# Hybrid decoder layer on one core: the mixing part with its norms, splits, meta columns and order of work rewritten

## The chip, the core and the metric

The kernel runs on one core of a Trainium2 chip. The metric is the device time of one execution in microseconds, given as the median of several runs; the times are from the device. TensorE (PE) multiplies matrices, VectorE (DVE) and ScalarE (ACT) work element by element, GpSimd (POOL) can do element work too and issues some transfers, SyncE (SP) issues most transfers. Each engine executes its own instructions in order and waits for the others by semaphores.

## The reference

One decoder layer over 512 tokens of width 1024, with 16 learned meta tokens in front (528 rows). What is computed:

```python
h = layer_norm(concat([meta, x]), ln_in_g, ln_in_b)
q, k, v, gb, gc, z = split(h @ w_in)            # 512 columns each
attn = differential_attention(q, k, v)          # 4 heads, two softmax maps each, causal, T5 bias
conv = gb * short_conv(gc * z, conv_w)          # depthwise, width 3, causal
mix = concat([attn, conv]) @ w_out
h = layer_norm(ALPHA * h + mix, ln1_g, ln1_b)
ffn = peer(h, w_q, sub_keys, u, v)              # per token and head: top-16 of 128 x 2 sub-keys, then experts
out = layer_norm(ALPHA * h + ffn, ln2_g, ln2_b)[16:]
```

A head's attention is softmax(map 0) - lam * softmax(map 1), times v, then an RMS norm over 128 columns. The expert stage (`peer`) needs the queries of all tokens and two top-16 selections per token and head before it can gather or weigh experts.

## The kernel before

All products are done in float16 with a high and a low half per operand: `split` writes the high half by ScalarE (`hi = scale * src`) and the low half by VectorE (`lo = scale * src - hi`); `mm3` then multiplies three times (high-high, high-low, low-high) into one PSUM bank. `split_pool` is a second form, with two ScalarE passes and the low half on GpSimd; `load_w(..., pool=True)` uses it for the four chunks (0.5 MB each) of a weight of 512 columns. Weights are split into three rotating pairs of buffers, so a weight's split can begin once the third one before it has been used up.

The order of the work: the Python program below gives each engine its instructions with a priority by program order, and a planner, which works with estimated durations, fixes the order on every engine before the run. An engine never departs from that order on the chip.

- Entry: `tile_v` for the four row tiles of 128 tokens and the 16 meta rows (i = -1): `layer_norm`, `split_rows`, transposes into `tTh`/`tTl` (`rows_to_T`), product with the value weight. Then the key and the query projections.
- Loop: 16 `units` (4 row blocks i x 4 heads h). Per unit `att_a` (scores of both maps, bias, maximum, exponentials, split into `ph` and `pl`), run two units ahead; `att_t` (transposes of the probabilities); one `fill` (a quarter of `conv_gc`, `conv_z` or `conv_gb`, or an output projection); `att_b` (times values, norm); `att_c` one unit later (transposes into `mixh`/`mixl`). The meta columns have operands of their own: 16-column transposes into `pTm`, 16-row products with `vmh`/`vml`.
- After the loop: output projections of row blocks 2 and 3 with a norm each (`out_proj`), transposes (`out_T`), the load of the first query weight of the expert stage and its product, first for 384 tokens, then for the last 128.
- Expert stage: three more query weights, sub-key scores, 64 runs of `top16` on VectorE, then the products with all experts' `u`, and at the end with all `v`. The first row tile's experts are gathered row by row through GpSimd's queue; its last norm is `layer_norm(x1[0], ...)`.

In `layer_norm` the statistics give mean and variance, `rstd` takes the power on GpSimd and one refinement step on VectorE; the normalization is one pass (VectorE, or ScalarE where `act_norm`), then times g on VectorE, then plus b (GpSimd where `pool_add`).

Of the kernel before, what the change touches and what calls it, by code (L numbers as in the profile page):

```python
# [23 lines left out]
H = 4  # L24
# [28 lines left out]
def build(tc, A, out):  # L53
# [35 lines left out]
    def layer_norm(x, n, g, b, pool_add, act_norm=False, halves=None):  # L89
        stt = small.tile([P, 2, 6], F32, name="bst")  # L90
        mv = small.tile([P, 2], F32, name="bmv")
        for c in range(2):
            V.bn_stats(stt[:n, c, :], x[:n, c * 512:(c + 1) * 512])
        V.bn_aggr(mv[:n], stt[:n])
        r = rstd(mv[:n, 1:2], n, EPS)
        if halves:
            for c in range(2):
                cs = slice(c * 512, c * 512 + 512)
                y = x[:n, cs]
                V.tensor_scalar(y, y, mv[:n, 0:1], r[:n], op0=OP.subtract, op1=OP.mult)  # L100
                V.tensor_tensor(y, y, g[:n, cs], op=OP.mult)
                V.tensor_tensor(y, y, b[:n, cs], op=OP.add)
                halves(cs)
            return
# [21 lines left out]
    def split_rows(x, n, pool, lo_eng):  # L126
# [3 lines left out]
        lo_eng.tensor_tensor(xl[:n], x[:n], xh[:n], op=OP.subtract)  # L130
# [9 lines left out]
    def load_w(src, nb, pool=False):  # L140
        wh = wst.tile([P, KT, 512], F16, name="wh")
        wl = wst.tile([P, KT, 512], F16, name="wl")
        for j in range(4):
# [3 lines left out]
            (split_pool if pool else split)(wh[:, s, :], wl[:, s, :], w, WS)  # L147
# [18 lines left out]
    with ExitStack() as s1:  # L166
# [21 lines left out]
        vmh = q.tile([NM, T], F16, name="vmh")  # L188
        vml = q.tile([NM, T], F16, name="vml")
# [13 lines left out]
        def tile_v(i):  # L203
# [3 lines left out]
            if i == 0:  # L207
# [7 lines left out]
                layer_norm(x, n, *lnv, pool_add=False, halves=half)  # L215
                rows_to_T((xh, xl), n, r0)
            else:
                layer_norm(x, n, *lnv, pool_add=i > 1, act_norm=i > 0)
                rows_to_T(split_rows(x, n, wk, G if i > 1 else V), n, r0)
# [5 lines left out]
            wv = W["v"]  # L225
            p = bank()
            mm3(p[:n], lambda k: tTh[:, k, r0:r0 + n], lambda k: tTl[:, k, r0:r0 + n],
                lambda k: wv[0][:, k, :], lambda k: wv[1][:, k, :], KT)
            if i < 0:
                split(vmh, vml, p[:n], 1.0 / WS)  # L230
            else:
                split(vh[:, i, :], vl[:, i, :], p[:n], 1.0 / WS)
# [48 lines left out]
        def conv_gc(c):  # L281
            if c == 0:
                W["gc"] = load_w(A["w_in"], 4, pool=True)
# [3 lines left out]
        def conv_z(c):  # L287
            if c == 0:
                W["z"] = load_w(A["w_in"], 5, pool=True)
# [4 lines left out]
        def conv_gb(c):  # L294
            if c == 0:
                W["gb"] = load_w(A["w_in"], 3, pool=True)
# [8 lines left out]
        def out_proj(i, nb):  # L305
            for b in range(2):
                if ("wo", b) not in W:
                    W["wo", b] = load_w(A["w_out"], b, pool=True)
# [20 lines left out]
        def att_a(i, h):  # L329
# [4 lines left out]
            for m in range(2):  # L334
                r = slice(m * DK, (m + 1) * DK)
                for f0 in range(0, w, 512):
                    f1 = min(w, f0 + 512)
                    p = bankA()
# [549 lines left out]
```

## Time and profile before

| | us |
|---|---|
| median of 3 runs | 1536.63 (1535.18 to 1537.24) |
| the profiled execution | 1538.28 |
| its span, first to last instruction | 1536.5 |
| busy in the span: PE / DVE / ACT / POOL | 1427.5 / 1220.7 / 749.5 / 376.5 |

Times in rows are microseconds from the start of the span, if no unit stands there. A busy TensorE is not TensorE at its peak: its instructions overlap, so a product's own duration is longer than its distance to the next one. Idle time before an instruction stands in brackets with what ended it.

### The profile page before, as it was taken

What the parts mean: (1) busy time and instruction counts of PE and PEld (TensorE: products, weight loads), DVE (VectorE), ACT (ScalarE), POOL (GpSimd) and SP (SyncE); (2) the same over time, 40 slices, a digit from 0 to 9 for tenths busy, and PEclk for the clock granted to TensorE, in tenths of its full rate; (3) what the DMA queues carried; (4) which work ended last, traced back from release to release, by engine and by line L of the source; (5) the groups of instructions that cost most, each with busy time, mean ns of one, the idle gap of its engine ahead of it and who ended that gap; (6) DMA issues with size and microseconds to landing.
All of it is one profiled execution on the core that took longest, in us unless ns stands there. A gap on an engine that the chain in (4) does not pass through costs nothing.

```text
span 1536.5 us, 23225 instructions
## 1 busy us (share of the span) xinstructions
PE 1427.5 (93%) x8768; PEld 764.4 (50%) x8768; DVE 1220.7 (79%) x2509; ACT 749.5 (49%) x1227; POOL 376.5 (25%) x262
## 2 busy tenths in 40 slices
PE   5799999969989979897999999999999999999994
PEld 2244545554555647574454545545455555555551
DVE  8414678649899999894788898888978888988886
ACT  5427546363245838474444444444544444444441
POOL 2334432342001223101022122222312122212213
PEclk9799999989999989999999999999999999999997
DMA  6352111070035757759899889899989999999851
GB/s 229 111 159 69 57 55 56 1 236 15 1 114 168 249 179 251 240 173 336 334 364 384 322 352 359 352 357 349 371 338 351 357 353 342 373 353 357 321 213 55
DMA packets 85989, 370.92 MB, mean 241 GB/s; under 512 B 10495, under 2 KB 15647, under 8 KB 69492
## 3 DMA queue, kind: packets, MB, share of 16 engines
q1 hardware_dynamic: 57724, 200.53, 35.9%
q0 software_dynamic: 28144, 168.90, 30.0%
q8 instruction: 68, 1.11, 0.3%
q14 instruction: 45, 0.37, 0.1%
q10 hardware_dynamic: 8, 0.01, 0.0%
HBM read 335.05 MB, written 35.69 MB: 241 GB/s over the span
## 4 chain that ended last, share of the span: by engine, by line
PE 33%; issue 21%; DVE 9%; POOL 4%; DMA 3%; POOLq 0%; ACT 0%; DVEq 0%
PE po L816 19%; PE pa L154 13%; POOL grow L671 3%; DMA grow<-peer_uv,idx 3%; DVE ul L116 2%; DVE rh L651 1%; DVE rl L652 1%; DVE oh L650 1%; DVE oh L649 1%; POOL gscr L638 1%; PE b L628 0%; DVE tci L163 0%; DVE c L161 0%; DVE tci L160 0%; DVE soh L583 0%
## 5 line engine op out<-in xcount | busy, mean ns | idle before, releaser
L154 PE MATMUL pa<-tTh,uh 128*128 128x384 f16 x1024 | 338.0, 330 | 8.9 <-ACT act L484 8.5
L154 PE MATMUL pa<-tTh,ul 128*128 128x384 f16 x1024 | 337.7, 330 | 8.8 <-DVE ul L116 8.8
L154 PE MATMUL pa<-tTl,uh 128*128 128x384 f16 x1024 | 337.6, 330 | 0.0
L671 POOL DMA_INDIRECT grow<-peer_uv,idx x128 | 175.6, 1372 | 611.0 <-DVE acc L688 546.0
L154 PEld LDWEIGHTS <-uh 128*128 128x128 f16 x2048 | 201.2, 99 | 148.8 <-issue 16.2
L116 DVE SCALAR_TENSOR_TENSOR ul<-uf,uh 128x1024 f16<-128x1024 f32 x128 | 161.8, 1264 | 100.6 <-ACT uh L115 100.5
L816 PEld LDWEIGHTS <-wwh 128*128 128x128 f16 x1488 | 145.8, 98 | 182.2 <-ACT wwh L808 12.6
L115 ACT ACTIVATE uh<-uf 128x1024 f16<-128x1024 f32 x128 | 135.2, 1056 | 202.3 <-PE pa L154 185.7
L816 PE MATMUL po<-pvh,wwh 128*128 128x512 f16 x744 | 182.1, 381 | 11.8 <-ACT pvh L115 11.1
L816 PE MATMUL po<-pvl,wwh 128*128 128x512 f16 x744 | 181.6, 380 | 0.0
L816 PE MATMUL po<-pvh,wwl 128*128 128x512 f16 x744 | 180.8, 379 | 0.0
L116 DVE SCALAR_TENSOR_TENSOR pvl<-vf,pvh 128x1024 f16<-128x1024 f32 x128 | 155.6, 1220 | 26.1 <-ACT pvh L115 26.1
L115 ACT ACTIVATE pvh<-vf 128x1024 f16<-128x1024 f32 x128 | 134.3, 1050 | 70.5 <-PE po L816 69.8
L688 DVE SCALAR_TENSOR_TENSOR acc<-grow,gact,acc 128x1024 f32<-128x1024 f32 x127 | 162.6, 1280 | 0.6 <-ACT gact L680 0.6
L678 DVE SCALAR_TENSOR_TENSOR grow<-grow,x 128x1024 f32<-128x1024 f32 x128 | 156.2, 1220 | 7.7 <-DMA grow<-peer_uv,idx 7.7
L154 PEld LDWEIGHTS <-ul 128*128 128x128 f16 x1024 | 101.2, 99 | 78.8 <-DVE ul L116 11.1
L808 ACT ACTIVATE wwh<-w 128x384 f16<-128x384 f32 x128 | 66.7, 522 | 142.4 <-DVE w L806 142.4
L154 PE MATMUL b<-tTh,wh 128*128 128x512 f16 (+4 forms) x416 | 122.8, 321 | 13.0 <-DVE tTh L138 10.5
L154 PE MATMUL b<-tTl,wh 128*128 128x512 f16 (+4 forms) x416 | 124.2, 320 | 0.0
L154 PE MATMUL b<-tTh,wl 128*128 128x512 f16 (+4 forms) x416 | 123.7, 319 | 0.0
L816 PEld LDWEIGHTS <-wwl 128*128 128x128 f16 x744 | 72.8, 98 | 87.8
L154 PEld LDWEIGHTS <-wh 128*128 128x128 f16 x832 | 69.9, 100 | 75.4 <-issue 17.4
(228 smaller groups left out, 2039.7 us busy)
## 6 DMA issues: line engine op xcount, KB each, us to landing
uf<-uT SPq DMA_DIRECT2D x128, 512.0 KB
vf<-vL SPq DMA_DIRECT2D x128, 512.0 KB
gscr<-stg POOLq DMA_DIRECT2D x12, 2048.0 KB, 13.3
gr<-gscr SPq DMA_DIRECT2D x32, 768.0 KB
w<-w_in SPq DMA_DIRECT2D x24, 512.0 KB
w<-w_q SPq DMA_DIRECT2D x16, 512.0 KB
ascr<-act POOLq DMA_DIRECT2D x18, 384.0 KB, 4.8
aload<-ascr SPq DMA_DIRECT2D x18, 384.0 KB
```

What stands on the lines that cost most here:

```text
L115: S.activation(hi, src, AF.Copy, scale=scale)
L116: V.scalar_tensor_tensor(lo, src, scale, hi, op0=OP.mult, op1=OP.subtract)
L154: m = PE.matmul(o, a(k), b(k), start=first and n == 0, stop=last and n == 3 * nk - 1)
L638: G.dma_start(gscr[:, :, (i - 1) * (P // CT) + c, :], stg.rearrange("p (g j) t -> p g (j t)", j=GG))
L649: V.tensor_tensor(pairs(o2), row, mid(gT[:, 1, ts]), op=OP.is_equal)
L650: V.tensor_tensor(pairs(o1), row, mid(gT[:, 0, ts]), op=OP.is_equal)
L651: V.tensor_tensor(pairs(rh), pairs(o2), mid(gT[:, 2, ts]), op=OP.mult)
L671: G.indirect_dma_start(out=uv, out_offset=None, in_=A["peer_uv"], in_offset=bass.IndirectOffsetOnAxis(ap=idx[:, j:j + 1], axis=0))
L678: V.scalar_tensor_tensor(uv[:, :D], uv[:, :D], 1.0, x1[0], op0=OP.mult, op1=OP.mult, accum_out=c)
L688: V.scalar_tensor_tensor(acc, uv[:, D:], c, acc, op0=OP.mult, op1=OP.add)
L808: S.activation(wh, w, AF.Copy)
L816: PE.matmul(po[i][c], x[:, ts], y[:, c * 512:(c + 1) * 512], start=f and k == 0, stop=False)
```

## The change

`layer_norm` becomes two VectorE passes, (x - mean) * g and then * rstd + b, on VectorE everywhere. `split_pool` goes: all weights are split by `split`, and the low halves of the rows and of the probabilities are taken on VectorE. GpSimd keeps the power in `rstd` and its transfers.

The 16 meta columns of a unit become one tile of 128 columns: both maps, each with (high, low) twice; one transpose gives `pTm`, and one product per map with `vm`, a zero-padded tile of 128 rows that holds the meta values' high and low halves at the matching rows (the meta rows' value product is made for 8 copies of the 16 rows, `xrep`). Scores are issued with the two maps in turn, with a bank from the second pool for columns from 512 on. `fill` is written out anew: two quarters of `conv_gc`/`conv_z` in each of the first four units, `conv_gb` in the next four, then the output projections of blocks 0, 1 and 2; the last half of the query product is put around the last output projection, and the load of the first query weight is written into unit 10.

```diff
-    def layer_norm(x, n, g, b, pool_add, act_norm=False, halves=None):
+    def layer_norm(x, n, g, b, halves=None):
...
+        for c in range(2) if halves else (None,):
+            cs = slice(0, D) if c is None else slice(c * 512, c * 512 + 512)
+            y = x[:n, cs]
+            V.scalar_tensor_tensor(y, y, mv[:n, 0:1], g[:n, cs], op0=OP.subtract, op1=OP.mult)
+            V.scalar_tensor_tensor(y, y, r[:n], b[:n, cs], op0=OP.mult, op1=OP.add)
+            if halves:
                 halves(cs)
-        if act_norm:
-            mr = small.tile([P, 1], F32, name="mr")
-            V.scalar_tensor_tensor(mr[:n], mv[:n, 0:1], -1.0, r[:n], op0=OP.mult, op1=OP.mult)
-            S.activation(x[:n], x[:n], AF.Identity, bias=mr[:n], scale=r[:n])
-        else:
-            V.tensor_scalar(x[:n], x[:n], mv[:n, 0:1], r[:n], op0=OP.subtract, op1=OP.mult)
-        V.tensor_tensor(x[:n], x[:n], g[:n], op=OP.mult)
-        (G if pool_add else V).tensor_tensor(x[:n], x[:n], b[:n], op=OP.add)
...
-    def split_pool(hi, lo, src, scale):
-        S.activation(src, src, AF.Copy, scale=scale)
-        S.activation(hi, src, AF.Copy)
-        G.tensor_tensor(lo, src, hi, op=OP.subtract)
...
-            (split_pool if pool else split)(wh[:, s, :], wl[:, s, :], w, WS)
+            split(wh[:, s, :], wl[:, s, :], w, WS)
...
+        vm = q.tile([P, H, 2, P], F16, name="vm")
+        V.memset(vm, 0.0)
...
+            if i < 0:
+                a, b = (wk.tile([P, KT, P], F16, name=f"xrep{e}", tag=t) for e, t in enumerate(("xh", "xl")))
+                for d, s in ((a, tTh), (b, tTl)):
+                    S.copy(d.rearrange("p k (r t) -> p k r t", t=NM),
+                           s[:, :, :NM].unsqueeze(2).to_broadcast([P, KT, P // NM, NM]))
...
+                for m in range(2):
+                    o = lambda r: vm[r, :, m, :]
+                    f = lambda r: p[r].rearrange("p (h d) -> p h d", h=H)
+                    r = slice(m * 64, m * 64 + 64)
+                    S.activation(o(r), f(r), AF.Copy, scale=1.0 / WS)
+                    r = slice(m * 64 + 32, m * 64 + 64)
+                    V.scalar_tensor_tensor(o(r), f(r), 1.0 / WS, o(r), op0=OP.mult, op1=OP.subtract)
...
-                last = i >= 2
-                layer_norm(x1[i], P, *lnv, pool_add=not last, act_norm=not last)
-                W["x", i] = split_rows(x1[i], P, wk, V if last else G)
+                layer_norm(x1[i], P, *lnv)
+                W["x", i] = split_rows(x1[i], P, wk)
...
+            for f0 in range(0, w, 512):
+                f1 = min(w, f0 + 512)
+                ps = [bankA() if f0 == 0 else bank() for _ in range(2)]
+                for e, (a, b) in enumerate(((qh, kh), (qh, kl), (ql, kh))):
+                    for r, p in zip(rs_, ps):
+                        PE.matmul(p[:, :f1 - f0], a[r, h, qs], b[r, h, f0:f1], start=e == 0, stop=e == 2)
...
-            S.activation(ph[:, :, :w], lg[:, :, :w], AF.Copy)
-            G.tensor_tensor(pl[:, :, :w], lg[:, :, :w], ph[:, :, :w], op=OP.subtract)
+            lm = lg[:, :, :NM].unsqueeze(2).to_broadcast([P, 2, 2, NM])
+            S.activation(pm[:, :, :, 0, :], lm, AF.Copy)
+            V.tensor_tensor(pm[:, :, :, 1, :], lm, pm[:, :, :, 0, :], op=OP.subtract)
+            S.activation(ph[:, :, :w - NM], lg[:, :, NM:w], AF.Copy)
+            V.tensor_tensor(pl[:, :, :w - NM], lg[:, :, NM:w], ph[:, :, :w - NM], op=OP.subtract)
...
-                    PE.transpose(tm[:NM, a, m, :], s[:, m, :NM], ident)
...
-            S.copy(pTm, tm[:NM, :2])
+            tm = bank(F16)
+            PE.transpose(tm[:, :P], pm.rearrange("p m r a t -> p (m r a t)"), ident)
+            S.copy(pTm, tm[:, :P])
...
-                mm3(o, lambda k: pTm[:, 0, m, :], lambda k: pTm[:, 1, m, :],
-                    lambda k: vmh[:, hs], lambda k: vml[:, hs], 1, last=False)
+                PE.matmul(o, pTm, vm[:, h, m, :], start=True, stop=False)
...
+        conv = [(f, c) for f in (conv_gc, conv_z, conv_gb) for c in range(4)]
+        fill = [conv[2 * n:2 * n + 2] for n in range(4)] + [[c] for c in conv[8:]]
+        fill += [[(out_proj, 0, 0)], [(out_proj, 0, 1)], [(out_proj, 1, 0)],
+                 [(out_proj, 1, 1), (out_T, 0)], [(out_T, 1)], [(out_proj, 2, 0)], [(out_proj, 2, 1)], []]
...
+            if n == 10:
+                wqs[0] = load_w(A["w_q"], 0)
...
-        for i in range(2, NT):
-            for nb in range(2):
-                if (i, nb) == (NT - 1, 0):
-                    att_c(*units[-1])
-                out_proj(i, nb)
-            out_T(i - 1)
-        wqs = {0: load_w(A["w_q"], 0)}
...
-        pq_mm(wqs[0], pq0, 0, 384)
+        out_T(2)
+        pq_mm(wqs[0], pq0, 0, 384, (0, 1))
+        att_c(*units[-1])
+        out_proj(3, 0)
+        out_proj(3, 1)
+        pq_mm(wqs[0], pq0, 0, 384, (2, 3))
         out_T(NT - 1)
         pq_mm(wqs[0], pq0, 384, 512)
```

## Rows read from the trace of the kernel before

**Rows 1.** Stretches: length; PE, PEld, DVE, ACT, POOL busy; clock, DMA share, GB/s.

```profile
0.00:117.00 117.00, 87.85 (x492) 39.34 (x492) 54.72 (x97) 50.70 (x64) 39.17 (x25) 0.90 0.51 164
117.00:307.70 190.70, 182.81 (x1418) 95.62 (x1418) 126.38 (x352) 106.69 (x203) 72.52 (x53) 0.96 0.15 48
307.70:346.30 38.60, 26.54 (x241) 19.29 (x240) 18.46 (x21) 23.34 (x27) 16.71 (x10) 0.87 0.71 235
346.30:440.90 94.60, 91.35 (x573) 48.40 (x573) 89.27 (x532) 29.70 (x59) 10.09 (x6) 1.00 0.06 18
440.90:700.00 259.10, 236.36 (x1876) 154.55 (x1875) 248.73 (x611) 164.28 (x203) 48.51 (x31) 0.95 0.65 209
```

**Rows 2.** Timeline of TensorE, one unit of two blocks: start, us, line, operation, count.

```profile
177.43 0.22 PE L154 MATMUL b<-vmh,pTm 16*128 16x128 f16 x1
...
178.76 0.28 PE L402 MATMUL bh<-ident,ohl 128*128 128x128 f16 x2
...
179.58 0.22 PE L364 MATMUL bh<-ident,ph 128*16 128x128 f16 x1
...
180.97 0.17 PE L154 MATMUL b<-tTh,wh 128*128 128x2 f16 x1
```

**Rows 3.** Timeline of TensorE: score products of both maps, blocks 2 and 3.

```profile
178.96 0.35 PE L154 MATMUL pa<-kh,qh 64*128 64x400 f16 x2
...
255.40 0.39 PE L154 MATMUL pa<-kh,qh 64*128 64x512 f16 x1
...
257.54 0.39 PE L154 MATMUL pa<-kh,qh 64*128 64x512 f16 x1
```

**Rows 4.** VectorE, single lines in the loop: duration ns min/median/max, first and last start.

```profile
L116 DVE SCALAR_TENSOR_TENSOR wl<-w,wh x4: 1201/1222/2425, 243.9 to 254.8; 128x1024 f16<-128x1024 f32 x4
...
L84 DVE SCALAR_TENSOR_TENSOR rt<-ry,ve x19: 210/220/2077, 135.9 to 299.5; 128x1 f32<-128x1 f32 x19
...
L299 DVE SCALAR_TENSOR_TENSOR y<-gc,cw,y x4: 748/750/2357, 169.5 to 240.2; 128x512 f32<-128x512 f32 x4
```

**Rows 5.** Timelines of GpSimd and of VectorE around 164.

```profile
163.87 2.13 POOL L121 TENSOR_TENSOR wl<-w,wh 128x1024 f16<-128x1024 f32 x1
...
163.93 2.08 DVE L84 SCALAR_TENSOR_TENSOR rt<-ry,ve 128x1 f32<-128x1 f32 x1 [0.81 <-POOL ry L83]
```

**Rows 6.** VectorE's groups in the loop: busy us, mean ns, idle before, releaser.

```profile
L84 DVE SCALAR_TENSOR_TENSOR rt<-ry,ve 128x1 f32<-128x1 f32 x19 | 7.9, 414 | 8.7 <-POOL ry L83 8.6
...
L395 DVE TENSOR_TENSOR ohl<-o,ohl 128x128 f16<-128x128 f32 x16 | 6.1, 380 | 4.1 <-ACT ohl L394 3.7
...
L383 DVE RECIPROCAL rz<-z 128x2 f32<-128x2 f32 x16 | 2.6, 163 | 4.3 <-ACT lg L347 4.2
```

**Rows 7.** Timelines of TensorE and VectorE in the hand-over.

```profile
310.24 0.81 PE L154 MATMUL b<-tTh,wh 128*128 128x384 f16 x4 [1.50 <-ACT tTh L138]
...
325.84 0.61 PE L137 MATMUL bh<-ident,xh 128*128 128x128 f16 x8
...
335.51 1.23 DVE L116 SCALAR_TENSOR_TENSOR ul<-uf,uh 128x1024 f16<-128x1024 f32 x1 [4.40 <-ACT uh L115]
336.65 0.68 DVE L138 COPY tTh<-bh 128x1024 f16<-128x1024 f16 x1
...
337.39 1.01 PE L154 MATMUL b<-tTh,wh 128*128 128x128 f16 x5 [10.50 <-DVE tTh L138]
...
346.32 0.49 DVE L159 MAX8 svt<-sc 128x8 f32<-128x128 f32 x2 [1.33 <-ACT sc L531]
```

**Rows 8.** Timeline of VectorE: eviction and split of row tile 2.

```profile
296.52 0.69 DVE L315 SCALAR_TENSOR_TENSOR x<-b,x 128x512 f32<-128x512 f32 x1 [2.27 <-PE b L154]
...
304.72 1.21 DVE L130 TENSOR_TENSOR xl<-x,xh 128x1024 f16<-128x1024 f32 x1
```

**Rows 9.** Timelines of GpSimd and ScalarE in the entry.

```profile
44.52 8.24 POOL L130 TENSOR_TENSOR xl<-x,xh 128x1024 f16<-128x1024 f32 x1 [1.17 <-ACT xh L129]
...
72.01 0.59 ACT L115 ACTIVATE vmh<-b 16x512 f16<-16x512 f32 x1 [4.25 <-PE b L154]
```

More of the change, by code (lines that the diff above doesn't have):

```diff
@@ L213, in half @@
                     V.tensor_tensor(xl[:, cs], x[:, cs], xh[:, cs], op=OP.subtract)
-                layer_norm(x, n, *lnv, pool_add=False, halves=half)
+                layer_norm(x, n, *lnv, halves=half)
                 rows_to_T((xh, xl), n, r0)
             else:
-                layer_norm(x, n, *lnv, pool_add=i > 1, act_norm=i > 0)
-                rows_to_T(split_rows(x, n, wk, G if i > 1 else V), n, r0)
+                layer_norm(x, n, *lnv)
+                rows_to_T(split_rows(x, n, wk), n, r0)
             if "v" not in W:
@@ L333, in att_a @@
             qs = slice(i * P, (i + 1) * P)
[L334 to L338, printed above, removed]
-                    mm3(p[:, :f1 - f0], lambda k: qh[r, h, qs], lambda k: ql[r, h, qs],
-                        lambda k: kh[r, h, f0:f1], lambda k: kl[r, h, f0:f1], 1)
+            rs_ = [slice(m * DK, (m + 1) * DK) for m in range(2)]
+            for f0 in range(0, w, 512):
[4 more added lines that the diff above has]
+                        PE.matmul(p[:, :f1 - f0], a[r, h, qs], b[r, h, f0:f1], start=e == 0, stop=e == 2)
+                for m, p in enumerate(ps):
                     V.scalar_tensor_tensor(lg[:, m, f0:f1], p[:, :f1 - f0], DK ** -0.5,
@@ L348, in att_a @@
                              accum_out=z[:, m:m + 1])
[L349 to L353 removed]
+            ph = wk.tile([P, 2, T], F16, name="ph", bufs=3)
+            pl = wk.tile([P, 2, T], F16, name="pl")
+            pm = wk.tile([P, 2, 2, 2, NM], F16, name="pm", bufs=3)
+            lm = lg[:, :, :NM].unsqueeze(2).to_broadcast([P, 2, 2, NM])
[3 more added lines that the diff above has]
+            V.tensor_tensor(pl[:, :, :w - NM], lg[:, :, NM:w], ph[:, :, :w - NM], op=OP.subtract)
+            pp_[i, h] = ph, pl, pm, z
         def att_t(i, h):
             nb = i + 1
[L357 removed]
+            ph, pl, pm, z = pp_.pop((i, h))
             pT = wk.tile([P, 2, 2, NT, P], F16, name="pT")
[L359 to L360 removed]
+            pTm = wk.tile([P, P], F16, name="pTm")
             for a, s in enumerate((ph, pl)):
@@ L406, in build @@
         units = [(i, h) for i in range(NT) for h in range(H)]
-        fill = [(f, (c,)) for f in (conv_gc, conv_z, conv_gb) for c in range(4)]
-        fill += [(out_proj, (0, 0)), (out_proj, (0, 1)),
-                 (out_proj, (1, 0)), (lambda: (out_proj(1, 1), out_T(0)), ())]
+        conv = [(f, c) for f in (conv_gc, conv_z, conv_gb) for c in range(4)]
+        fill = [conv[2 * n:2 * n + 2] for n in range(4)] + [[c] for c in conv[8:]]
+        fill += [[(out_proj, 0, 0)], [(out_proj, 0, 1)], [(out_proj, 1, 0)],
+                 [(out_proj, 1, 1), (out_T, 0)], [(out_T, 1)], [(out_proj, 2, 0)], [(out_proj, 2, 1)], []]
+        wqs = {}
         att_a(*units[0])
@@ L415, in build @@
             att_t(*u)
-            if fill:
-                f, args = fill.pop(0)
+            for f, *args in fill[n]:
                 f(*args)
+            if n == 10:
+                wqs[0] = load_w(A["w_q"], 0)
             att_b(*u)
@@ L421, in build, with pq_mm @@
                 att_c(*units[n - 1])
-        for i in range(2, NT):
-            for nb in range(2):
-                if (i, nb) == (NT - 1, 0):
-                    att_c(*units[-1])
-                out_proj(i, nb)
-            out_T(i - 1)
-        wqs = {0: load_w(A["w_q"], 0)}
-        pq0 = [bank() for _ in range(4)]
-        def pq_mm(w, pq, r0, r1):
-            for c in range(4):
+        pq0 = [None] * 4
+        def pq_mm(w, pq, r0, r1, cc=range(4)):
+            for c in cc:
+                if pq[c] is None:
+                    pq[c] = bank()
                 cs = slice(c * P, (c + 1) * P)
@@ L514, in build @@
             else:
-                pq = [bank() for _ in range(4)]
+                pq = [None] * 4
                 pq_mm(w, pq, 0, 512)
```

42 lines of the change are left out of this document (13 added, 29 removed).

## The prediction

> **What bounds the kernel now.** I read the table by stretches first. [rows 1] splits the span where the work changes: the entry up to the last key and query projection (0 to 117), the loop over the 16 attention units with convolution and output projection (to 307.7, the end of the last output projection), the hand-over to the retrieval queries (to 346.3, when the first top-16 starts), the top-16 stage (to 440.9), and the stretch behind it up to 700, where the work changes again and which the diff hardly touches. The reader is to see that TensorE is busy 182.8 of 190.7 us in the loop, VectorE only 126.4 and GpSimd 72.5; that in the hand-over nobody is full; and that in the top-16 stage TensorE (91.4 of 94.6) and VectorE (89.3) are both nearly full. Behind it VectorE is busy 248.7 of 259.1 us, and nothing there can begin before the top-16 values exist: so I take it that whatever is gained or lost up to 440.9 moves the end by as much.
>
> Three kinds of loss show in the first 346 us, and the instruction timelines show them. First, TensorE pays for small tiles. In one unit with two key blocks the product with the values runs from 177.43 to 178.76, 1.33 us for 18 products, and the transposes from 179.58 to 180.97, 1.39 us for 12, though two 128-column products there take 0.28 where one takes 0.22, so a pitch of 0.056 [rows 2]. The difference lies around the 16-row and 16-column operands. Second, GpSimd holds up VectorE: a one-element instruction at 163.93 lasts 2.08 us while GpSimd's subtraction (163.87, 2.13 us) runs, against a median of 0.22 [rows 4, 5]; and GpSimd's own subtraction at 44.52 takes 8.24 us [rows 9]. Third, an order: at 326 the last rows are transposed, but their copy (336.65) stands on VectorE behind a weight split (335.51) that itself waited 4.40 us, and TensorE idles 10.50 us before 337.39 [rows 7].
>
> **Entry (0 to 117).** The two-pass norm replaces, for tiles 2, 3 and the meta rows, passes spread over ScalarE, VectorE and GpSimd; row splits go to VectorE. The 8.24 us subtraction becomes one VectorE instruction of about 1.21 us (same size as the median split in [rows 4]), 7 us earlier for tile 3's transposes. Against it: two ScalarE copies that repeat the meta columns, about 1 us each, behind which the meta product waits, partly under tile 3's product; the meta product itself keeps its 24 products of 512 columns. The zeroing of the new value tile lies in the start, when VectorE waits for the input. Another 1 us comes from the shorter chain of tile 1. The last meta product, evicted at 72.01 [rows 9], comes about 8 us earlier, and the projections behind it are pure TensorE work. Bounds: 0, and -15, half of the 29 us that TensorE is idle there [rows 1]. I take -8, nearest to the 7 of the row.
>
> **Loop (117 to 307.7).** TensorE: the meta columns as one tile turn 18 products into 14 and 12 transposes into 9 for two blocks: 14 x 0.056 = 0.78 for 1.33, 9 x 0.056 = 0.50 for 1.39, so 1.44 us per unit and 23 us for 16. (The counts removed, 4 and 3, and the operand switches are the same for any number of blocks.) The alternating score maps give less than they seem to: already now the two maps start as a pair (0.35 us for two at 178.96), except in the last four units, where the first map's 512 columns begin at 255.40 and the second's at 257.54 [rows 3]. There three products of 0.22 become free: 0.65 us x 4 = 2.6. TensorE's floor is 190.7 - 26 = 165 us.
>
> VectorE gets what GpSimd loses. Splits of three weights (the third convolution weight and two output weights, four chunks each) 12 x 1.21 = 14.5; the first query weight's four are on VectorE already [rows 4]. The low half of the probabilities, 256 to 1024 elements by block: between 0.22 (one element) and 1.21 (1024) that is 0.46, 0.71, 0.96, 1.21, times four units each: 13.4. The small meta subtraction, 16 x 0.22 = 3.5. Norms behind the output projection: tiles 0 and 1 get two passes of 1.22 for one pass and a small instruction, and a split of 1.21, +4.6 together; tile 2 goes from 3.26 to 2.44, -0.8. Sum +35.2. Off goes the hold-up: in two groups alone, the 19 instructions of line 84 (mean 414 against a median of 220 ns, 3.7 us) and the four of line 299 (one of 2357 against 750, 1.6), it is 5.3 us [rows 4, 6]; I take -12 for all groups, a bit over twice that, as GpSimd keeps only one one-column power per norm of its 72.5. VectorE then has 126.4 + 35.2 - 12 = 150.
>
> [...]
>
> 150 on VectorE and 165 on TensorE would still fit side by side, but they don't lie evenly. The convolutions now come two at a time in the first four units: about 53 us of TensorE, with some 34 of VectorE. That leaves TensorE 112 and VectorE 116 for the other twelve units and the last projections. VectorE's queue is in order, and three waits stay in it: for GpSimd's power 8.6 us, for ScalarE's half 3.7 and its exponentials 4.2 [rows 6], 16.5, three quarters of it in these units: 116 + 12 = 128. So 53 + 128 = 181, a gain of 10; what is late next is VectorE. Bounds: -26 (TensorE's floor) and +5 (only 5 of hold-up back, no wait hidden). I take -10.
>
> **Hand-over (307.7 to 346.3).** Now half of the first query product, 48 products, stands ahead of the last unit's projection and half behind. From 310.24 to 325.84 is 15.6 for 96, so 7.8 each. Behind the last projection: the chain from eviction to the split runs 296.52 to 305.93 for tile 2, 9.4 us [rows 8], less 0.8 for the two-pass norm and less 0.7 for a foreign instruction inside: 7.9, under the 7.8 of product. Then transposes 0.9, two copies 1.3, and from the product's start to the first top-16 8.9 (337.39 to 346.32) [rows 7]: with the half's small surplus 19.5. If the other half and the second transposition (8.7 + 1.5 wait) aren't covered by VectorE's lag in the loop, 29.7. The stall need not go: the query weights' splits are on VectorE too now, also ahead of that copy. Bounds: -19 (19.5) and 0 (38.6, the stall as it was); I take 29.7, so -9.
>
> **Top-16 (346.3 to 440.9).** The last query weight's splits (four GpSimd instructions lie here now) cost VectorE 4 x 1.21 = 4.8, less about 1 of hold-up; 5.3 us of VectorE idle time take some. Bounds 0 and +14.5, if all twelve splits fall in here. I take +3.
>
> **After that.** The first tile's last norm loses a GpSimd pass and gains about 0.4 us of VectorE, ahead of the final rows: 0, bounds -2 and +2. Other stretches 0.
>
> Sum: -8 - 10 - 9 + 3 = -24. The profiled execution took 1538.28 us for its span of 1536.5; after, 1514.3 for 1512.5. The median of the runs is 1.65 below the profiled one: 1536.63 - 24 = **1512.6 us**.
>
> **Rivals.** (a) VectorE keeps up, its work falling into TensorE's shade: loop -26, hand-over -12, entry -8, top-16 +1, together -45: 1491.6. For it: 64 us of VectorE idle in the loop; against it: the 128 above. (b) Gains eaten: VectorE becomes the bound (loop -2), the copy again waits behind splits (hand-over 0), entry -8, top-16 +5: -5, 1531.6. For it: one queue has all the small steps. (c) Slower: the queue of VectorE in the hand-over. If the eight splits of two query weights stand ahead of the last transposes' copies and wait for their transfers (the window already moves 235 GB/s, so 2.2 us a chunk of 0.5 MB, 18 us in place of the 10.5 stall), +8 there, the third's and late ones +14.5 in the top-16 stage, loop 0, entry -8: +14.5, 1551.1. It decides once more than four splits precede the copy. Against it: splits come early when their buffers are free.
>
> [...]
>
> **How the numbers follow.** Likeliest 55%, (a) 14%, (b) 19%, (c) 9%, (d) 3%. Its own range is 1500 to 1526. The 80% range is 1494 to 1535: it leaves out half of (a), and (c) and (d). A measurement can tell about 0.2% (3 us) from no change. Faster: 55 + 14 + 12 of (b) = 81%; same: 6%, of (b); slower: 13%, (c), (d) and 1 of (b).
>
> **What would show it.** Right: a meta product evicted near 64; no 16-row products; VectorE near 150 us in the loop and fuller than TensorE in units 4 to 15, with TensorE waiting on its results; the first top-16 near 319; top-16 stage 97 us; no VectorE instruction stretched to 2 us. Wrong: TensorE still full through all units (a), the last copies behind splits (b, c), a clock well under 0.96 in the loop (d), or a different length of the stretches behind, which I hold fixed.

## The result and the profile after

The changed kernel takes 1525.36 us in the median of 4 runs (1525.21 to 1525.47), the kernel before 1536.93 beside it: a ratio of 0.9921 with a 95% interval of 0.9905 to 0.9937, a gain of 11.6 us. The profiled execution took 1525.31 us for a span of 1523.5, 13.0 less than the span before. Forecast was 24.

The table by stretches of the changed kernel, cut at the same events as [rows 1] (first score product, eviction of the last output projection, first top-16, end of the top-16 stage); its columns are those of [rows 1]:

```profile
0.00:106.60 106.60, 85.45 (x493) 38.59 (x494) 62.62 (x105) 44.98 (x59) 11.94 (x14) 0.95 0.54 185
106.60:303.20 196.60, 174.64 (x1375) 98.27 (x1375) 141.36 (x402) 86.57 (x201) 13.33 (x19) 0.92 0.15 47
303.20:328.80 25.60, 18.32 (x182) 13.54 (x181) 17.10 (x24) 12.79 (x17) 1.52 (x1) 0.87 0.77 261
328.80:427.70 98.90, 92.20 (x565) 49.04 (x563) 93.30 (x537) 29.29 (x58) 1.49 (x2) 0.98 0.10 35
```

The entry is 10.4 us shorter, the loop 5.9 longer, the hand-over 13.0 shorter, the top-16 stage 4.3 longer: together -13.2 at 427.7, and the rest of the span keeps it (1095.6 us behind that point before, 1095.8 after). The loop now holds some work that stood in the hand-over before, the third block's transposes and half of the first query product, 8.7 us by [rows 7]. Like for like the loop gained 2.8 and the hand-over 4.3.

Timelines of the changed kernel, TensorE (PE), VectorE (DVE) and ScalarE (ACT), from the meta value product over the start of the loop and one unit of two blocks to the hand-over:

```profile
62.41 0.59 ACT L227 ACTIVATE vm<-b 64x512 f16<-64x512 f32 x1 [6.89 <-PE b L139]
...
107.57 1.23 DVE L106 SCALAR_TENSOR_TENSOR wl<-w,wh 128x1024 f16<-128x1024 f32 x1 [4.73 <-ACT wh L105]
...
109.32 3.49 DVE L106 SCALAR_TENSOR_TENSOR wl<-w,wh 128x1024 f16<-128x1024 f32 x3
112.72 0.52 DVE L340 SCALAR_TENSOR_TENSOR lg<-pa,bias 128x144 f32<-128x144 f32 x2
...
113.07 0.28 PE L338 MATMUL pa<-kh,qh 64*128 64x144 f16 x1 [6.11 <-DVE lg L340]
...
185.67 0.40 PE L367 MATMUL bh<-ident,ph 128*128 128x128 f16 x4
...
186.39 0.38 PE L139 MATMUL b<-tTh,wh 128*128 128x512 f16 x1
...
191.57 0.22 PE L381 MATMUL b<-vm,pTm 128*128 128x128 f16 x1
...
192.30 0.22 PE L139 MATMUL b<-vh,pT 128*128 128x128 f16 x1
...
303.21 0.69 DVE L314 SCALAR_TENSOR_TENSOR x<-b,x 128x512 f32<-128x512 f32 x1
...
304.76 1.22 DVE L106 SCALAR_TENSOR_TENSOR wl<-w,wh 128x1024 f16<-128x1024 f32 x1
...
307.02 1.23 DVE L106 SCALAR_TENSOR_TENSOR wl<-w,wh 128x1024 f16<-128x1024 f32 x1 [0.91 <-ACT wh L105]
...
308.22 1.28 DVE L99 SCALAR_TENSOR_TENSOR x<-x,bmv,lnv 128x1024 f32<-128x1024 f32 x1
...
310.08 1.22 DVE L106 SCALAR_TENSOR_TENSOR wl<-w,wh 128x1024 f16<-128x1024 f32 x1
...
311.28 1.21 DVE L106 SCALAR_TENSOR_TENSOR wl<-w,wh 128x1024 f16<-128x1024 f32 x1
...
312.60 1.28 DVE L100 SCALAR_TENSOR_TENSOR x<-x,ry,lnv 128x1024 f32<-128x1024 f32 x1
315.00 1.23 DVE L115 TENSOR_TENSOR xl<-x,xh 128x1024 f16<-128x1024 f32 x1 [1.12 <-ACT xh L114]
```

The reader is to see three things. The small tiles came out nearly as priced: for two blocks the products with the values begin at 191.57 and the last of the 14 at 192.30 (0.78 us with its pitch, 1.33 in [rows 2]), and from the first transposes to the next product are 0.72 us (1.39 in [rows 2], 0.50 forecast), so 1.22 us a unit for a forecast of 1.44. At the start of the loop four weight splits stand on VectorE between 107.57 and 112.72, ahead of the first scores, and TensorE waits 6.11 us. And in the hand-over four splits (line 106) stand inside the norm of the last row block; from its eviction at 303.21 to the end of its split at 316.23 are 13.0 us.

The clock behind the wait at 113.07, in a table of three short stretches, and then the loop up to the fourth unit's result (170.1) and from there to the first query product (columns as above, the granted clock is the third number from the end):

```profile
106.60:113.10 6.50, 0.39 (x8) 0.25 (x9) 5.53 (x7) 4.26 (x5) 0.00 (x0) 0.87 0.42 123
113.10:117.00 3.90, 3.05 (x42) 1.95 (x42) 3.60 (x14) 3.20 (x15) 0.00 (x0) 0.50 0.89 321
117.00:121.00 4.00, 4.00 (x11) 1.38 (x10) 1.56 (x8) 1.57 (x7) 0.00 (x0) 0.50 0.03 11
...
106.60:170.10 63.50, 56.23 (x481) 29.47 (x482) 32.44 (x98) 24.06 (x67) 1.65 (x3) 0.92 0.20 67
170.10:283.40 113.30, 98.61 (x795) 58.61 (x792) 102.84 (x298) 58.35 (x130) 11.68 (x16) 0.92 0.12 38
```

Behind 6.1 us of standing still TensorE is granted half its clock (0.50 in both stretches from 113.10 to 121.00) for the next eight microseconds.

The single lines that answer to [rows 4], in the loop of the changed kernel (minimum, median and maximum in ns):

```profile
L84 DVE SCALAR_TENSOR_TENSOR rt<-ry,ve x19: 214/219/222, 133.1 to 281.5; 128x1 f32<-128x1 f32 x19
...
L106 DVE SCALAR_TENSOR_TENSOR wl<-w,wh x20: 1204/1221/1226, 107.6 to 302.1; 128x1024 f16<-128x1024 f32 x20
```

No VectorE instruction of the loop is stretched to 2 us any more; the longest takes 1.28 us.

### The profile page after: what moved, and what is told of

Its sections match the earlier page's. It is cut to its first block, busy times and chain, and to the rows that moved or that the text cites. A ratio compares the mean times of both kernels' runs of the same rounds, so it can differ in the third digit from the quotient of the medians.

```text
span 1523.5 us, 22944 instructions
## 1 busy us (share of the span) xinstructions
PE 1405.7 (92%) x8656; PEld 759.8 (50%) x8656; DVE 1247.0 (82%) x2573; ACT 712.6 (47%) x1209; POOL 281.1 (18%) x205
## 4 chain that ended last, share of the span: by engine, by line
PE 47%; DVE 21%; issue 19%; DMA 7%; POOL 4%; ACT 1%; POOLq 0%; SPq 0%; DVEq 0%; ACTq 0%
PE po L821 21%; PE pa L139 13%; PE b L139 12%; DMA grow<-peer_uv,idx 4%; DVE ul L106 2%; POOL grow L676 2%; DVE wl L106 2%; DMA gscr<-stg 1%; DVE rh L656 1%; POOL ry L83 1%; DVE rl L657 1%; DVE oh L654 1%; DMA kf<-keysT 1%; DVE oh L655 1%; POOL gscr L643 1%
## 5 line engine op out<-in xcount | busy, mean ns | idle before, releaser
L676 POOL DMA_INDIRECT grow<-peer_uv,idx x128 | 192.0, 1500 | 594.1 <-DVE acc L693 535.3
L821 PEld LDWEIGHTS <-wwh 128*128 128x128 f16 x1488 | 145.7, 98 | 181.5 <-ACT wwh L813 12.2
```

The source lines that it names most:

```text
L676: G.indirect_dma_start(out=uv, out_offset=None, in_=A["peer_uv"], in_offset=bass.IndirectOffsetOnAxis(ap=idx[:, j:j + 1], axis=0))
L821: PE.matmul(po[i][c], x[:, ts], y[:, c * 512:(c + 1) * 512], start=f and k == 0, stop=False)
```

## The experiments

All comparisons are ratios to the kernel before on the same chip; the medians in us that the text gives come from several chips, on which the kernel before took 1536.9 to 1538.0. The stretches are those of the first table, in us, from one profiled execution of each: the same entry code differs by up to 3.8 us between them, so a difference of that size in a single stretch is no finding by itself. "Old order" means the order of the kernel before, with all other parts of the change.

| kernel | ratio (95%) | entry | loop | hand-over | top-16 |
|---|---|---|---|---|---|
| before | 1 | 117.0 | 190.7 | 38.6 | 94.6 |
| changed | 0.9921 (0.9905-0.9937) | 106.6 | 196.6 | 25.6 | 98.9 |
| before + meta tile | 0.9957 (0.9944-0.9970) | 114.4 | 182.4 | 38.6 | 95.1 |
| before + new order | 1.0079 (1.0062-1.0096) | 116.6 | 213.7 | 26.9 | 96.1 |
| before + norm, no GpSimd | 0.9885 (0.9870-0.9899) | 104.8 | 188.6 | 32.6 | 95.7 |
| changed, old order | 0.9779 (0.9763-0.9794) | 106.9 | 170.4 | 33.0 | 97.1 |
| changed, one convolution quarter per unit | 0.9924 (0.9906-0.9941) | 106.8 | 195.9 | 25.1 | 98.3 |
| changed, query product in one piece | 0.9875 (0.9858-0.9892) | 103.2 | 188.7 | 33.0 | 95.7 |
| old order, convolution crowded | 0.9889 (0.9871-0.9907) | 104.2 | 186.6 | 32.7 | 96.7 |
| old order, product in two pieces | 0.9808 (0.9795-0.9821) | 107.0 | 181.1 | 22.5 | 100.2 |
| old order, bias early | 0.9845 (0.9831-0.9858) | 119.3 | 168.6 | 32.2 | 95.7 |
| old order, maps one by one | 0.9808 (0.9794-0.9821) | 105.5 | 172.8 | 31.6 | 97.3 |
| changed, third weight on GpSimd | 0.9976 (0.9965-0.9986) | 105.5 | 202.6 | 25.4 | 98.7 |
| changed, query weights on GpSimd | 0.9891 (0.9872-0.9910) | 105.4 | 195.6 | 24.5 | 96.1 |
| changed, third weight behind the scores | 0.9917 (0.9902-0.9932) | 105.3 | 191.9 | 25.2 | 98.5 |
| changed, query weights behind the copies | 0.9886 (0.9871-0.9900) | 106.7 | 195.9 | 20.6 | 99.9 |
| old order, third weight behind | 0.9760 (0.9741-0.9779) | 105.4 | 168.0 | 33.1 | 97.2 |
| old order, both behind | 0.9759 (0.9742-0.9776) | 104.2 | 166.3 | 30.0 | 97.5 |

Theory at the outset: the missing half is weight splits on VectorE that stand ahead of what TensorE waits for. Rivals: the small tiles are worth less than priced; the new order costs what the other parts give.

### The parts one by one

The kernel before with one part of the change each: the meta tile (with its subtraction on VectorE), the new order, the norm and the subtractions on VectorE.

```diff
+            lm = lg[:, :, :NM].unsqueeze(2).to_broadcast([P, 2, 2, NM])
+            PE.matmul(o, pTm, vm[:, h, m, :], start=True, stop=False)
```

> The kernel before with the meta columns as one tile and nothing else of the change (its small subtraction on VectorE, the large one on GpSimd as before). Theory of the prediction: TensorE is full in the loop, its busy time there falls by 23 us and the loop by 15 to 23: about 1517 us. Rival: the steps of a unit on VectorE, ScalarE and GpSimd set the pace as soon as TensorE is a little faster, the loop falls by 10 us or less: 1527 us or more.

```diff
+        fill = [conv[2 * n:2 * n + 2] for n in range(4)] + [[c] for c in conv[8:]]
+        pq_mm(wqs[0], pq0, 0, 384, (0, 1))
```

> The kernel before with the new order alone (two convolution quarters in each of the first four units, the query product around the last projection, its weight loaded from unit 10 on). Theory of the prediction: only the hand-over gains, by 9 us or less, as TensorE was full in the loop: 1528 to 1532 us. Rival: GpSimd's splits of the early query weight fall into the loop and delay the probabilities' low halves: 1537 us or more.

```diff
-            G.tensor_tensor(pl[:, :, :w], lg[:, :, :w], ph[:, :, :w], op=OP.subtract)
+            V.tensor_tensor(pl[:, :, :w], lg[:, :, :w], ph[:, :, :w], op=OP.subtract)
```

> The kernel before with the norm in two VectorE passes and no GpSimd arithmetic, with the old order and the old meta tiles. Theory of the prediction: the entry falls by 8 us; in the loop VectorE, near 147 us, stays under TensorE's 183: 0; the hand-over and the top-16 stage lose 3 to 8 by the query weights' splits: 1529 to 1536 us. Rival: VectorE's splits stand ahead of what TensorE needs in the loop already: 1540 us or more.

Measured: -0.43%, +0.79%, -1.15%. The sum, -0.79%, is what the whole change gave, but by luck: the parts don't add up. Without the new order the rest of the change, the alternating maps included, gave -2.21% (next section) where these two sum to -1.58%, and on top of the rest the new order costs 1.42 points where it costs 0.79 alone. The tables by stretches of the three loops, in that order:

```profile
114.40:296.80 182.40, 163.41 (x1309) 89.76 (x1309) 134.34 (x368) 102.20 (x219) 71.37 (x53) 0.93 0.16 50
```

```profile
116.60:330.30 213.70, 198.81 (x1483) 105.76 (x1483) 131.67 (x353) 108.33 (x205) 74.66 (x54) 0.93 0.14 44
```

```profile
104.80:293.40 188.60, 181.34 (x1433) 95.92 (x1433) 141.57 (x384) 90.75 (x185) 13.36 (x19) 0.96 0.15 48
```

With the meta tile TensorE is busy 19.4 us less than in [rows 1] and the loop falls by only 8.3: the rival's case. The new order alone lengthens the loop by 23, 14 more than the work moved into it, where I had expected none; the whole costs 12 us. That is the rival's number, but not its way: TensorE waits 1.2 us for GpSimd in that loop and 5.4 for VectorE's scores. The norm and the subtractions gained 17 us where I had expected 1 to 8, mostly in the entry (-12.2) and the hand-over (-6.0), 2.1 in the loop.

### The order

```diff
-        fill = [conv[2 * n:2 * n + 2] for n in range(4)] + [[c] for c in conv[8:]]
+        fill = [(f, (c,)) for f in (conv_gc, conv_z, conv_gb) for c in range(4)]
...
-        pq_mm(wqs[0], pq0, 0, 384, (0, 1))
-        att_c(*units[-1])
```

> The changed kernel with the old order of convolution, projection and query product and its other parts kept. Theory: the two convolution quarters in each of the first four units take TensorE's cover away from the other twelve, where the small steps on VectorE then set the pace; with an even order TensorE stays full and the gains of the other parts add up: norm and no GpSimd arithmetic alone gave -17, the meta tile alone -7, so about 1513 us, between 1508 and 1517. Rival: without GpSimd VectorE bounds the loop in any order once TensorE's 23 us are off, so the meta tile adds nothing: 1519 to 1524 us.

1505.38 us (1502.03 to 1505.68): 20 us faster than the change as made, below even the range expected. The order is the loss. This version has the same 6.11 us wait and the same low clock at the start of its loop (0.74 from 110 to 130 in both), and yet a loop of 170.4 us, so the splits ahead of the first scores are not what separates the two. Which piece of the order it is was asked three times. The changed kernel with the crowding (two convolution quarters in each of the first four units) taken out, the tail (the query product around the last output projection) kept (the load of the first query weight moves to unit 15):

```diff
+        fill = [[c] for c in conv]
+        fill += [[(out_proj, 0, 0)], [(out_proj, 0, 1)], [(out_proj, 1, 0)], [(out_proj, 1, 1), (out_T, 0)]]
...
+        out_T(1)
+        out_proj(2, 0)
+        out_proj(2, 1)
         out_T(2)
```

> The changed kernel with its new tail (query product around the last output projection), but one convolution quarter in each of the first twelve units and the output projections of blocks 0 and 1 in the last four. Theory that the crowded first units are the loss: about as with the old order throughout, 1508 to 1517 us, TensorE full in the middle of the loop. Rival that the tail is the loss (the query weights' splits in the last norm): as the changed kernel, 1522 to 1528 us.

1527.22 us, a miss, and a fault of the experiment. Its waits of TensorE from 240 to 330 (in total, times, longest):

```profile
PE bh L122 <- ACT xh L114: 15.9, 3, 6.6
```

I had put the transposes of two row blocks right behind the norms that feed them, and TensorE stood still for each (4.86 and 6.59 us; the third wait, 4.47, is the one that the changed kernel has too). Its time says nothing on crowding, but the middle of its loop does: there it runs as the old-order version does. Both from 200 to 220, this run first:

```profile
200.00:220.00 20.00, 16.17 (x145) 9.52 (x143) 19.83 (x50) 13.19 (x26) 1.10 (x2) 1.00 0.17 53
```

```profile
200.00:220.00 20.00, 16.18 (x145) 9.54 (x144) 19.90 (x51) 12.82 (x26) 0.64 (x2) 1.00 0.17 53
```

Its sixteenth unit's result comes 148.5 us behind the first score product, 148.9 in the old-order version. The tail alone was undone next:

```diff
-        pq_mm(wqs[0], pq0, 0, 384, (0, 1))
         att_c(*units[-1])
         out_proj(3, 0)
         out_proj(3, 1)
-        pq_mm(wqs[0], pq0, 0, 384, (2, 3))
+        pq_mm(wqs[0], pq0, 0, 384)
```

> The changed kernel with its new filling of the units, but the query product behind the last output projection as a whole. Theory that the crowded first units are the loss: within 4 us of the changed kernel's 1525.4. Rival that the tail is the loss: 1518 us or less.

1519.04 us, between the two. Loop and hand-over together stay (221.7 against 222.2); 3.2 lie in the top-16 stage and 3.4 in the entry, whose code is the same. Last, the crowding alone, put into the version with the old order:

```diff
-        fill = [(f, (c,)) for f in (conv_gc, conv_z, conv_gb) for c in range(4)]
+        fill = [conv[2 * n:2 * n + 2] for n in range(4)] + [[c] for c in conv[8:]] + [[]] * 4
```

> The version with the old order (1505.4 us) with one thing of the new order: two convolution quarters in each of the first four units, so that the third convolution's quarters lie in units 4 to 7, nothing in units 8 to 11, the output projections where the old order has them. Theory that the crowding is the loss: VectorE waits for TensorE in the first units (11.7 and 8.5 us ahead of the first two unit results, as in the changed kernel) and sets the pace afterwards: +10 to +18, 1515 to 1523 us. Rival that the loss lies in the projections of block 2 among the units and their norms and splits: within 4 us, 1502 to 1509 us.

1518.89 us, +13.5 by the medians and 1.1 points by the ratios, as the theory said; its loop is 16.2 us longer. What is left of the 20 us lies in the rest of the order; undoing the tail gave 6.3, but half of it in the entry, which the tail doesn't touch, so its place stays open. VectorE's waits for TensorE from 106 to 150 (in total, times, longest), with the crowding and without:

```profile
DVE o L389 <- PE b L139: 19.3, 2, 10.7
```

```profile
DVE o L389 <- PE b L139: 10.8, 4, 5.9
```

Stretches of 20 us in the middle of the loop, with the crowding and without:

```profile
150.00:170.00 20.00, 20.00 (x168) 10.67 (x167) 11.59 (x36) 6.77 (x17) 1.10 (x2) 1.00 0.17 54
...
190.00:210.00 20.00, 16.45 (x113) 9.12 (x113) 18.35 (x57) 12.82 (x28) 1.45 (x3) 0.82 0.09 28
210.00:230.00 20.00, 15.08 (x124) 8.79 (x122) 17.06 (x60) 10.87 (x28) 1.30 (x3) 0.76 0.00 1
```

```profile
150.00:170.00 20.00, 19.98 (x185) 11.30 (x184) 18.07 (x60) 9.76 (x29) 1.10 (x2) 1.00 0.31 96
...
190.00:210.00 20.00, 17.95 (x150) 10.27 (x149) 19.69 (x56) 8.90 (x22) 1.65 (x3) 1.00 0.09 27
210.00:230.00 20.00, 16.36 (x153) 9.88 (x151) 19.90 (x51) 12.98 (x25) 0.55 (x1) 1.00 0.25 79
```

TensorE is full in the first units either way; what the crowding takes away is VectorE's work there (11.59 against 18.07 us of 20). That work comes back in units whose filling is used up: TensorE then waits (15.08 of 20) and its granted clock is 0.76. How much of the 16.2 us is the clock and how much the waits isn't shown.

### The splits ahead of the scores and in the last norm

```diff
-                W["gb"] = load_w(A["w_in"], 3)
+                W["gb"] = load_w(A["w_in"], 3, pool=True)
```

> The changed kernel with the low halves of one weight, the third convolution weight, back on GpSimd. Theory: in the changed kernel its four splits (4 x 1.22 us, 107.6 to 112.8) stand on VectorE ahead of the first scores of the loop, TensorE waits 6.1 us there and works at half its clock for some us behind it; with them away about 5 us go: 1520 us, first score eviction right behind the last query split near 109, the granted clock near 0.95 in 110 to 120. Rival: VectorE sets the pace of the loop from the fifth unit on, and what is won at its start is lost by then or GpSimd's subtractions hold VectorE up again: 1524 to 1527 us.

```diff
-                wqs[nb + 1] = load_w(A["w_q"], nb + 1)
+                wqs[nb + 1] = load_w(A["w_q"], nb + 1, pool=True)
```

> The changed kernel with the low halves of the second to fourth query weight back on GpSimd. Theory: in the changed kernel five of these splits (1.22 us each) stand on VectorE inside the norm of the last row block, TensorE idles 4.7 us behind it at 315 and the top-16 stage carries four more: -5 in the hand-over, -3 in the top-16 stage, about 1518 us. Rival: GpSimd's subtractions, three to four times as long each and stretching VectorE's, come no earlier: 1524 us or more.

1533.55 and 1520.98 us: the first slower than the changed kernel, against theory and rival, the second faster by about 4. Neither tells the theory apart. On GpSimd the third weight's splits stood ahead of the loads of the bias, for which the first scores then waited; the second kernel's last norm was held up in another way. Timelines of GpSimd (POOL) and VectorE, first kernel, and of the same, second kernel:

```profile
106.60 6.28 POOL L111 TENSOR_TENSOR wl<-w,wh 128x1024 f16<-128x1024 f32 x3 [40.76 <-ACT wh L110]
112.82 2.19 POOL L259 DMA_DIRECT2D bias<-scr  x4
...
119.16 0.52 DVE L345 SCALAR_TENSOR_TENSOR lg<-pa,bias 128x144 f32<-128x144 f32 x2 [11.44 <-DMA bias<-scr]
```

```profile
296.95 9.37 POOL L111 TENSOR_TENSOR wl<-w,wh 128x1024 f16<-128x1024 f32 x4 [16.94 <-ACT wh L110]
306.28 0.55 POOL L83 TENSOR_TENSOR ry<-ve,mhalf 128x1 f32<-128x1 f32 x1
...
306.86 2.08 DVE L84 SCALAR_TENSOR_TENSOR rt<-ry,ve 128x1 f32<-128x1 f32 x1 [2.53 <-POOL ry L83]
...
309.16 1.86 DVE L86 TENSOR_TENSOR ry<-ry,rt 128x1 f32<-128x1 f32 x1
```

The norm's power waits behind 9.37 us of splits, and two one-element instructions are stretched to 2.08 and 1.86 us while two more splits run on GpSimd (4.21 us from 306.80), the hold-up of [rows 5]. GpSimd's splits took 2.1 to 2.3 us each there (4.21 for two, 9.37 for four), less than twice VectorE's 1.22 and not three to four times, and of the changed kernel's splits four, not five, stand inside that norm. The second kernel's gain of 4 us lies mostly in the top-16 stage (-2.8). Then the order alone was changed: the same splits on VectorE, queued behind the scores or behind the last copies.

```diff
+                with tc.issue_after(lgi[0, 1].ins):
+                    W["gb"] = load_w(A["w_in"], 3)
```

> The changed kernel with one edge of order: the four splits of the third convolution weight are queued on VectorE behind the scores of the second unit. Theory: TensorE's wait of 6.1 us at the start of the loop goes, and with it the missing part of the loop term: -5 to -6 against the changed kernel's 1525.4, about 1520 us. Rival: VectorE sets the pace from the fifth unit on and has to do the four splits anyway (4.9 us), so the gain is given back: 1524 to 1526 us.

```diff
+                with tc.issue_after(W["T", NT - 1].ins):
+                    wqs[nb + 1] = load_w(A["w_q"], nb + 1)
```

> The changed kernel with one edge of order: the splits of the second to fourth query weight are queued on VectorE behind the copies of the last transposes. Theory: the chain from the last projection's eviction to the copy falls from 13 us to 8, TensorE's 4.7 us wait at 315 goes, and what the top-16 stage gains in splits costs less than that: 1521 to 1523 us. Rival: the eight splits now fall into the top-16 stage, where VectorE is full (93 of 99 us): 8 x 1.2 = +10 there, against -5: 1526 to 1531 us.

The second, 1520.65 us, settles the hand-over: 25.6 to 20.6 us. VectorE's timeline in it:

```profile
302.61 0.69 DVE L315 SCALAR_TENSOR_TENSOR x<-b,x 128x512 f32<-128x512 f32 x1 [3.76 <-PE b L140]
...
309.14 1.23 DVE L115 TENSOR_TENSOR xl<-x,xh 128x1024 f16<-128x1024 f32 x1 [1.12 <-ACT xh L114]
310.86 0.69 DVE L123 COPY tTh<-bh 128x1024 f16<-128x1024 f16 x1 [0.49 <-PE bh L122]
...
312.06 4.62 DVE L106 SCALAR_TENSOR_TENSOR wl<-w,wh 128x1024 f16<-128x1024 f32 x4
```

From eviction to the end of the split are 7.8 us, against 13.0 in the changed kernel; the top-16 stage pays 1.0, and the median is 4.7 lower. The first, 1524.99 us (1519.76 to 1527.48), is not told apart from the changed kernel and lies where the rival said, though its profiled execution (1520.37, 4.6 under its own median) has the first scores' addition at 107.40 in place of 112.72 and a loop of 191.9 in place of 196.6. Its loop up to the fourth unit's result:

```profile
105.30:165.00 59.70, 55.26 (x481) 29.11 (x482) 31.80 (x98) 24.06 (x67) 1.65 (x3) 0.94 0.22 71
```

That is 59.7 us where the changed kernel took 63.5: the wait is worth 3.8 us there. The clock is low here too, behind waits of at most 2.06 us: 0.83 in the mean from 105.3 to 125, and the products of 512 columns start every 0.43 us from 112.9 to 115.4, against 0.22 ahead of the loop. So the stall's removal shows in a trace and not in the median; its worth for the whole stays open. On the version with the old order the same two edges gave:

> The version with the old order (1505.4 us) with the splits of the third convolution weight behind the second unit's scores, as in the run with the changed kernel. Theory: the wait at the start goes, -5: about 1500 us. Rival: VectorE's queue has no room later, 1504 to 1506 us.

> The same with the query weights' splits behind the copies of the last transposes as well. Theory: the hand-over falls by up to 5 us and the top-16 stage pays a part: 1497 to 1500 us. Rival: the splits cost more in the full top-16 stage than they free: 1501 us or more than the version without this edge.

1502.41 us (1496.86 to 1505.35) and 1498.89 (1496.11 to 1503.97). The first falls short of the theory's 1500 and its interval meets that of the old order; the second, with a hand-over of 30.0 in place of 33.1, is the fastest median, 0.9759, but not told apart from the first by its ratio.

### Three details of the old-order version

```diff
+        pq_mm(wqs[0], pq0, 0, 256)
         att_c(*units[-1])
...
+        pq_mm(wqs[0], pq0, 256, 384)
```

> The version with the old order (1505.4 us) with the query product of the first two row blocks put ahead of the last output projection, the other two behind it. Theory of the prediction's hand-over term: the last norm stays under nothing else than the third block's product, but what goes ahead covers the norm of block 2, so up to 5 us less, 1500 to 1505 us. Rival: the last norm, with the query weights' splits inside it (12 us), is left without cover when only a quarter of the product stands behind the projection: +3 to +8, 1508 to 1513 us.

1508.48 us. Loop and hand-over together are unchanged (203.6 against 203.4), the top-16 stage is 3.1 longer: the rival's size, not its place.

```diff
             tile_v(i)
+            if i == 0:
+                oh = wk.tile([NB + 1, RW], F32, name="bkt", tag="lg")
...
+                S.dma_start(drow, row)
```

> The version with the old order (1505.4 us) with the chain of the position bias (two small products, a row to memory, its spread copy, four loads) issued behind the first row tile in place of behind the meta rows. Theory: the four splits of the third convolution weight go ahead of the first scores only because the order takes the bias to be late; with the bias early the 6.1 us wait of TensorE at the start of the loop goes: 1499 to 1501 us. Rival: the splits stand there in any case, 1505 us, or the bias transfers delay the first weights: 1506 us or more.

1514.92 us. The wait at the start of the loop is down to 2.1 us and the loop 1.8 shorter (168.6 against 170.4), but the entry is 12.4 longer. TensorE's waits from 0 to 118:

```profile
PE bh L122 <- ACT xh L114: 15.4, 2, 15.0
```

One transpose waits 15.0 us for a row tile, whose norm (line 84) stands on VectorE behind splits that wait for their weight:

```profile
49.93 1.22 DVE L106 SCALAR_TENSOR_TENSOR wl<-w,wh 128x1024 f16<-128x1024 f32 x1 [3.20 <-ACT wh L105]
...
51.34 2.36 DVE L106 SCALAR_TENSOR_TENSOR wl<-w,wh 128x1024 f16<-128x1024 f32 x2
53.62 0.33 DVE L84 SCALAR_TENSOR_TENSOR rt<-ry,ve 128x1 f32<-128x1 f32 x2
```

The DMA share between 40 and 60 is 0.88 there and 0.65 without the edit, which fits the second rival.

```diff
+            for m in range(2):
+                mm3(p[:, :f1 - f0], lambda k: qh[r, h, qs], lambda k: ql[r, h, qs],
...
-                for e, (a, b) in enumerate(((qh, kh), (qh, kl), (ql, kh))):
```

> The version with the old order (1505.4 us) with the scores of one map behind those of the other, as in the kernel before. Theory of the prediction: alternating maps are worth 2.6 us of TensorE in the last four units: 1505 to 1508 us. Rival: they are worth more, as the sum of the meta tile (-7) and of the rest (-17) leaves some 8 us of the -32 without an owner: 1511 to 1514 us.

1507.53 us, +2.1 (loop +2.4), with intervals that just touch: the alternating maps are worth about the 2.6 us of the prediction, and not the rival's 6 to 9.

## Why the prediction was right or wrong

The sign and most of the mechanisms were right, the size was off by half: -13.0 in the profiled execution and -11.6 in the medians for a forecast of -24. Two terms of the sum were too large, the loop by 7.2 and the hand-over by 4.7 us, like for like.

**Entry, -8.** Measured -10.4; the norm and the subtractions alone gave -12.2. The last meta product's first eviction came at 62.41 where I wrote 64, and 72.01 in [rows 9].

**Loop, -10: the term that failed first.** The prediction's "So 53 + 128 = 181" was 63.5 and 124. The fourth unit's result is evicted at 170.1, 63.5 us behind the first score product: I had taken the first four units as TensorE at full speed with VectorE's work beside it, and it stood still for 6.1 us behind four of the splits, then ran at half clock (0.50) for eight. From 170.1 on it took 113.3 us up to the query product, and 11 more for the last projection: the 128 was near. VectorE was fuller than TensorE there, as forecast (102.8 and 98.6 of 113.3), and its total 141 where I wrote 150. The wait is not the whole of it. With the splits behind the scores the first four units still took 59.7 us: 3.8 of the 10.5 too much are the wait's. All of the rest lies ahead of the first unit's result, 20.3 us behind the first score product there, where the next three units take 13.1 each: TensorE is idle for 4.1 of the 20.3 and has a mean granted clock of 0.83. Whether that can be won back no run shows.

**Hand-over, -9: the second.** The step "the chain from eviction to the split ... 7.9, under the 7.8 of product" was 13.0, since four of the query weights' splits stood inside it. I had named that danger, but only for the copies, as a bound and in the rivals (b) and (c), not in the sum. With the splits queued behind the copies the chain took 7.8 us and the hand-over fell by 5.0, which covers the missing 4.7.

**Top-16 stage, +3.** Measured +4.3. **Behind it, 0.** Measured +0.2.

**Rivals.** (a), VectorE keeping up, asked for -26 in the loop; the old order gave -20 with the same VectorE work (141.1 us), so what separated my case from (a) was the order. I had priced the crowding inside my own case, 181 against TensorE's floor of 165, and crowding alone measured +16.2; but I never set it against the order that stood there, so I did not see that this part of the change was a loss. Alone the order cost 12 us, on top of the rest 20. (b), given 19%, came in two of its terms: the loop (-2 there, -2.8 measured) and the top-16 stage (+5, +4.3); in the hand-over it had 0 where 4.3 were gained. (c) did not come. Of (d), the clock, given 3%, only its sign came: the loop's clock is 0.92 where it was 0.96, with 0.50 behind the wait at 113.07 and 0.74 from 270 to 290, where TensorE is busy for 14.97 of 20 us. From 230 to 250, with 15.02 of 20, it is 0.95, and 0.76 in the crowded version with 15.08: what it goes by no run shows.

The hold-up, -12 on VectorE in the loop's term: the stretched instructions went (line 84's longest takes 0.22 us where it took 2.08), but with the norm and the subtractions alone the loop gained 2.1 us, the entry 12.2.

## What to carry to other kernels

When work moves to another engine, look at what each moved instruction stands ahead of in that engine's queue, and not only at the sum of busy time; four splits of 1.2 us each inside one chain cost 5 us on an engine that was busy for two thirds of that stretch (17.1 of 25.6). Filling work that is mostly TensorE's belongs evenly between units whose small steps fill VectorE (busy for 19.90 of 20 us from 210 to 230 in the old order): spending it early left the later units without cover here, and the loop took 16.2 us longer. A reordering is a part of a change with a price of its own, and an experiment that undoes it alone is the first to make.

## What the runs showed of the hardware that was not expected

The same entry code took 103.2 to 107.0 us in the profiled executions of thirteen kernels, and the stretch behind the top-16 stage, which no edit touches but for one norm, 1095.6 to 1100.5; the five runs of one kernel spread over up to 8.5 us (1496.86 to 1505.35, with a mean granted clock of 0.980 and 0.974). No run here tells why.

TensorE lost its clock at the start of the loop without a long wait, too: with the splits moved away its longest was 2.06 us there, and the products of 512 columns still started every 0.43 us from 112.9 to 115.4, twice the 0.22 ahead of the loop; the mean granted clock from 105.3 to 125 was 0.83.

With GpSimd's subtractions gone, more of TensorE's saving by the meta tile shows in the loop (188.6 to 172.8, -15.8) than with them (190.7 to 182.4, -8.3): norm, subtractions and meta tile together (old order, maps one by one) gave -1.92% where the two alone sum to -1.58%. Which step of a unit GpSimd held up isn't shown.
